# State space matrices prepared in six pieces on three engines, and all sines after the last table

## The chip, the cores and the metric

The kernel runs on one core of one Trainium2 chip. The metric is device time in microseconds for one launch, and the number given for the kernel is the median of several runs. Besides those runs there is one profiled execution, with its own time, from which every row below is taken.

## The reference

The reference is a network of two blocks over 256 tokens of width 1024, in float32. The first block has two layers, each a feed-forward part, a mixing part (two attentions and a pooling branch) and a second feed-forward part. The second block has an "even" layer with stick-breaking attention and a grouped state space mixer, and an "odd" layer with gated linear attention. Two parts matter here.

A feed-forward part (D_FF is 2816, so 22 chunks of 128 columns):

```
def swiglu(x, w_gate, w_up, w_down):
    return (jax.nn.silu(x @ w_gate) * (x @ w_up)) @ w_down
h = h + 0.5 * swiglu(rmsnorm(h, ffn2_norm[l]), ffn2_w_gate[l], ffn2_w_up[l], ffn2_w_down[l])
```

The parameters of the state space mixer, which depend on no token:

```
lam = lax.complex(lam_re, lam_im);  dt = jnp.exp(log_dt)[:, None]
lam_bar = jnp.exp(lam * dt)
b_bar = ((lam_bar - 1.0) / lam)[..., None] * bmat
```

## The kernel before, in words

Activations lie transposed: 128 features on the partitions, the 256 tokens in the free dimension. Every weight is fetched in tiles of 128x1024 float32, two per transfer of 1 MB on SyncE's queue (`ahead`, L295, three buffers named raw). `W` (L302) splits each tile for the matmuls: ScalarE copies it to the rounded format (L313, tile wh), VectorE writes the rest, source minus wh (L314, tile wl). Six buffers of wh and of wl let the split run ahead of TensorE. A product is then three matmuls (`mm3`, L317): high by high (L319), high by low (L320), low by high (L321).

`ffn` (L525) goes over the 22 chunks f. For a chunk, TensorE projects the gate and the up columns into one PSUM tile, psa for even f and psb for odd f, 24 matmuls each. Then a short chain makes the hidden chunk: VectorE multiplies the gate by the token scale (L581), ScalarE applies SiLU (L582), GpSimd multiplies by the halved scale (L583), VectorE multiplies by the up part (L584), and `split` makes the high (L332, ScalarE) and low (L333, VectorE) halves, tile hs. One chunk later TensorE multiplies hs by the down weights, 24 matmuls into psc. So a chunk is 72 matmuls on TensorE: the down product of chunk f-1, and the two projections of chunk f+1. Below, "the down product of chunk f" is named D and the number: D8 is that of chunk 8. It cannot start before L332 of chunk f has written hs.

In the last feed-forward part (f21), `ffn` also calls one step of a list at the head of each chunk from f = 1: `s5_prep` (L955) returns that list. It prepares what the even layer needs and what depends on parameters alone:

- `begin` (f = 1): three transfers and small columns of 128x16.
- `table` (f = 2 to 9): a table of angles, two groups at a time. VectorE L997 and L998, GpSimd L999, VectorE L1000, GpSimd L1001 and L1002, VectorE L1003 and L1004. Every second one ends with an absolute value on ScalarE (L1006), and its 512 columns are then a finished quarter of the table.
- `sines` (f = 10): three small sines (L1010 to L1012), the sine and cosine of each quarter (L1015, L1016), and a row of dependent 128x16 operations on GpSimd (L1017 to L1039), which give the columns cr, ci, lr and li.
- `outs` and `ins` (f = 11 and 12): 128x512 products of the matrices C and B with these columns, all on GpSimd (L1054 to L1086).
- `turned` (f = 13): eight transposes on TensorE (L1096) and two copies on ScalarE (L1097). `direct` (f = 14): 32 small matmuls (L1108, L1109) and four copies (L1112).

The order on an engine is not the order of the calls: a scheduler lists the instructions by their priority (the order of the calls) and by when it expects their inputs to be ready. Each engine then runs its own list strictly in that order, and an instruction that waits holds up all behind it on its engine. `issue_after` keeps what is traced in its block behind a given instruction of the same engine.

Of the kernel before, what the change touches and what calls it, by code (L numbers as in the profile page):

```python
# [12 lines left out]
AF = mybir.ActivationFunctionType  # L13
ALU = mybir.AluOpType
# [226 lines left out]
class Kern:  # L241
# [713 lines left out]
    def s5_prep(self):  # L955

        nc = self.nc
        g = nc.gpsimd
# [4 lines left out]
        tabs = []  # L963
        self.rho = rho2

        def view(t, m):
            return t.rearrange("p a t -> p (a t)").rearrange("p (m i t) -> p m i t", m=2, i=4)[:, m]
# [21 lines left out]
        def table(i):  # L989

            if i % 4 == 0:
                tabs.append(self.slot())
            sn = self.sin(i, 2).rearrange("p i t -> p (i t)")
            u, v, w = self.tmp(), self.tmp(), self.tmp()
            for m in range(2):
                h = slice(m * P, m * P + P)
                nc.vector.tensor_scalar(u[:, h], self.c("tidx"), ph[:, i + m:i + m + 1], None, ALU.mult)  # L997
                nc.vector.tensor_scalar(v[:, h], self.c("tidx"), pl[:, i + m:i + m + 1], None, ALU.mult)  # L998
            g.tensor_tensor(w, u, v, ALU.add)  # L999
            nc.vector.tensor_scalar(w, w, MAGIC, MAGIC, ALU.add, ALU.subtract)  # L1000
            g.tensor_tensor(u, u, w, ALU.subtract)  # L1001
            g.tensor_tensor(u, u, v, ALU.add)  # L1002
            nc.vector.tensor_scalar(u, u, 2 * math.pi, PI, ALU.mult, ALU.min)  # L1003
            nc.vector.tensor_scalar(sn, u, -PI, None, ALU.max)  # L1004
            if i % 4 == 2:
                nc.scalar.activation(view(tabs[-1], 1), view(tabs[-1], 0), AF.Abs)  # L1006

        def sines():
            with self.tc.issue_after(self.act.ins):
                nc.scalar.activation(sb, y, AF.Sin)  # L1010
                nc.scalar.activation(cb, ny, AF.Sin, bias=self.c("hpi"), scale=-1.0)
                nc.scalar.activation(sh, y, AF.Sin, scale=0.5)  # L1012
            for t in tabs:
                sn, cs = view(t, 0), view(t, 1)
                nc.scalar.activation(sn, sn, AF.Sin)  # L1015
                nc.scalar.activation(cs, cs, AF.Sin, bias=self.c("hpi"), scale=-1.0)  # L1016
            g.tensor_tensor(rho2, ea, ea, ALU.mult)  # L1017
            g.tensor_tensor(lr, ea, cb, ALU.mult)
            g.tensor_tensor(li, ea, sb, ALU.mult)

            g.tensor_scalar(em, ea, 1.0, None, ALU.add)
            g.tensor_tensor(em, em, th, ALU.mult)
            g.tensor_tensor(re, em, cb, ALU.mult)
            g.tensor_tensor(sh, sh, sh, ALU.mult)
            g.tensor_scalar(sh, sh, 2.0, None, ALU.mult)
            g.tensor_tensor(re, re, sh, ALU.subtract)
            g.tensor_tensor(im, ea, sb, ALU.mult)
            g.tensor_tensor(den, lre, lre, ALU.mult)
            g.tensor_tensor(t1, lim, lim, ALU.mult)
            g.tensor_tensor(den, den, t1, ALU.add)  # L1030
            nc.vector.reciprocal(den, den)
            g.tensor_tensor(cr, re, lre, ALU.mult)
            g.tensor_tensor(t1, im, lim, ALU.mult)
            g.tensor_tensor(cr, cr, t1, ALU.add)
            g.tensor_tensor(cr, cr, den, ALU.mult)
            g.tensor_tensor(ci, im, lre, ALU.mult)
            g.tensor_tensor(t1, re, lim, ALU.mult)
            g.tensor_tensor(ci, ci, t1, ALU.subtract)
            g.tensor_tensor(ci, ci, den, ALU.mult)  # L1039

        def wide(t):
            return t.rearrange("p a t -> p (a t)").rearrange("p (m i q) -> p m i q", m=2, i=16)

        def tile32():
            return self.tmp(512).rearrange("p (i q) -> p i q", i=16)

        def over(col):
            return col.unsqueeze(2).to_broadcast([P, 16, 32])

        def outs():  # L1050

            c0 = wide(self.s5c)
            t, t2 = tile32(), tile32()
            g.tensor_tensor(t, c0[:, 0], over(ci), ALU.mult)  # L1054
            g.tensor_tensor(t2, c0[:, 1], over(ci), ALU.mult)
            g.tensor_tensor(c0[:, 0], c0[:, 0], over(cr), ALU.mult)
            g.tensor_tensor(c0[:, 1], c0[:, 1], over(cr), ALU.mult)
            g.tensor_tensor(c0[:, 0], c0[:, 0], t2, ALU.subtract)
            g.tensor_tensor(c0[:, 1], c0[:, 1], t, ALU.add)
            g.tensor_scalar(c0[:, 1], c0[:, 1], -1.0, None, ALU.mult)  # L1060
            cs = [self.slot().rearrange("p a t -> p (a t)").rearrange("p (m i q) -> p m i q", m=2, i=16)
                  for _ in range(2)]
            neg, one, two, three = cs[0][:, 0], cs[0][:, 1], cs[1][:, 0], cs[1][:, 1]
            g.tensor_scalar(neg, c0[:, 0], -1.0, None, ALU.mult)
            t, t2 = tile32(), tile32()
            g.tensor_tensor(t, c0[:, 1], over(li), ALU.mult)
            g.tensor_tensor(t2, c0[:, 0], over(li), ALU.mult)
            g.tensor_tensor(one, c0[:, 0], over(lr), ALU.mult)
            g.tensor_tensor(two, c0[:, 1], over(lr), ALU.mult)
            g.tensor_tensor(one, one, t, ALU.add)  # L1070
            g.tensor_tensor(two, two, t2, ALU.subtract)
            g.tensor_scalar(three, one, -1.0, None, ALU.mult)
            self.cp = (one, two, three), (c0[:, 0], c0[:, 1], neg)

        def ins():

            n0 = wide(self.s5n)
            self.s5l = self.slot()
            l0 = wide(self.s5l)
            t, t2 = tile32(), tile32()  # L1080
            g.tensor_tensor(t, n0[:, 1], over(li), ALU.mult)
            g.tensor_tensor(t2, n0[:, 0], over(li), ALU.mult)
            g.tensor_tensor(l0[:, 0], n0[:, 0], over(lr), ALU.mult)
            g.tensor_tensor(l0[:, 1], n0[:, 1], over(lr), ALU.mult)
            g.tensor_tensor(l0[:, 0], l0[:, 0], t, ALU.subtract)
            g.tensor_tensor(l0[:, 1], l0[:, 1], t2, ALU.add)  # L1086

        def turned():

# [10 lines left out]
        def direct():  # L1100
# [11 lines left out]
                nc.scalar.activation(kt[q, :, q], ps[q].rearrange("p (c d) -> p c d", c=4), AF.Copy)  # L1112
            self.kt = kt

        return [begin] + [lambda i=i: table(i) for i in range(0, 16, 2)] + [sines, outs, ins, turned, direct]

    def even(self, h):

# [511 lines left out]
```

## Time and profile before

| what | value |
|---|---|
| runs | 1625.89, 1628.82, 1629.08 us; median 1628.82 us |
| profiled execution, its own time | 1626.93 us |
| its span, first to last instruction | 1625.2 us |
| VectorE, ScalarE, GpSimd busy | 64%, 50%, 24% of the span |
| mean granted TensorE clock | 0.994 |

The span is what the rows are drawn from; 1.73 us of the execution lie around it. In the rows TensorE is PE, VectorE DVE, ScalarE ACT and GpSimd POOL. Times in a timeline are from the span's start. The last feed-forward part lies at about 1060 to 1285 us, and the matrices are prepared in it.

### The profile page before, as it was taken

How to read it: one execution, taken by the hardware profiler on the slowest of the kernel's cores; microseconds unless marked ns; L12 is line 12 of the kernel's file. 1: busy time of each engine (PE TensorE's matmuls, PEld its weight loads, DVE VectorE, ACT ScalarE, POOL GpSimd, SP SyncE). 2: the span in 40 equal slices, each digit the busy share in tenths (PEclk: the TensorE clock that was granted, in tenths of full speed). 3: DMA queues.
4: the chain of work that ended last, by engine and by line, in shares of the span. 5: the costliest groups of instructions: out<-in, count | busy, mean ns of one | idle time of the engine just before them, and what ended most of it. 6: DMA issues, size and time to landing. Idle time of an engine off the chain costs nothing. (4 is left out here: it accounts for less than half of the span.)

```text
span 1625.2 us, 30427 instructions
## 1 busy us (share of the span) xinstructions
PE 1578.4 (97%) x12518; PEld 1506.2 (93%) x12518; DVE 1044.4 (64%) x1725; ACT 817.8 (50%) x1412; POOL 385.1 (24%) x446
## 2 busy tenths in 40 slices
PE   8999999999999999999999999999869999999998
PEld 8999998999999999999999899999869987998886
DVE  6655576676765557555576576776545687677643
ACT  6444455555544445444455565454434544566663
POOL 3111142002411113111141000453551111112232
PEclk9999999999999999999999999999989999999999
DMA  7555543334355554455544343554524433442530
GB/s 277 193 184 179 182 176 126 142 132 167 144 209 181 186 184 176 182 182 182 182 163 156 130 150 137 182 195 156 178 95 177 174 130 132 145 164 81 182 130 27
DMA packets 38459, 261.97 MB, mean 161 GB/s; under 512 B 4336, under 2 KB 5616, under 8 KB 7344
## 3 DMA queue, kind: packets, MB, share of 16 engines
q1 hardware_dynamic: 37440, 257.61, 44.1%
q0 software_dynamic: 736, 2.34, 0.5%
q8 instruction: 98, 1.61, 0.4%
q14 instruction: 41, 0.34, 0.1%
q10 hardware_dynamic: 144, 0.08, 0.0%
HBM read 258.96 MB, written 1.05 MB: 160 GB/s over the span
## 5 line engine op out<-in xcount | busy, mean ns | idle before, releaser
L314 DVE TENSOR_TENSOR wl<-raw,wh 128x1024 fp32r<-128x1024 f32 (+1 forms) x487 | 605.8, 1249 | 247.5 <-ACT wh L313 246.6
L313 ACT ACTIVATE wh<-raw 128x1024 fp32r<-128x1024 f32 (+1 forms) x487 | 508.2, 1049 | 449.2 <-PE psa L320 210.6
L319 PE MATMUL psa<-s,wh 128*128 128x256 f32 x1800 | 516.7, 288 | 2.0 <-ACT s L335 0.9
L320 PE MATMUL psa<-s,wh 128*128 128x256 f32 x1800 | 513.1, 285 | 4.9 <-DVE s L336 4.4
L321 PE MATMUL psa<-s,wl 128*128 128x256 f32 x1800 | 510.9, 284 | 0.2 <-DVE wl L314 0.2
L320 PEld LDWEIGHTS psa<-s,wh 128*128 128x128 f32 x1800 | 344.9, 192 | 11.1 <-DVE s L336 9.3
L319 PEld LDWEIGHTS psa<-s,wh 128*128 128x128 f32 x1800 | 344.6, 192 | 10.6 <-issue 5.4
L321 PEld LDWEIGHTS psa<-s,wl 128*128 128x128 f32 x1800 | 344.9, 192 | 2.0 <-issue 1.5
L583 POOL TENSOR_TENSOR t<-t,hrb 128x256 f32<-128x256 f32 x88 | 121.7, 1382 | 525.1 <-ACT t L582 525.1
L319 PE MATMUL psc<-hs,wh 128*128 128x256 f32 x704 | 200.7, 287 | 20.8 <-ACT hs L332 20.8
L319 PE MATMUL psb<-s,wh 128*128 128x256 f32 x752 | 213.9, 284 | 0.1
L321 PE MATMUL psb<-s,wl 128*128 128x256 f32 x752 | 213.2, 283 | 0.0
L320 PE MATMUL psb<-s,wh 128*128 128x256 f32 x752 | 213.1, 283 | 0.0
L320 PE MATMUL psc<-hs,wh 128*128 128x256 f32 x704 | 202.2, 288 | 2.9 <-DVE hs L333 2.1
L321 PE MATMUL psc<-hs,wl 128*128 128x256 f32 x704 | 200.5, 285 | 0.0
L319 PEld LDWEIGHTS psc<-hs,wh 128*128 128x128 f32 x704 | 136.0, 194 | 23.1 <-ACT hs L332 23.0
L319 PEld LDWEIGHTS psb<-s,wh 128*128 128x128 f32 x752 | 144.4, 192 | 0.6 <-ACT s L1097 0.3
L320 PEld LDWEIGHTS psb<-s,wh 128*128 128x128 f32 x752 | 144.4, 192 | 0.0
L321 PEld LDWEIGHTS psb<-s,wl 128*128 128x128 f32 x752 | 144.4, 192 | 0.0
L320 PEld LDWEIGHTS psc<-hs,wh 128*128 128x128 f32 x704 | 136.5, 194 | 5.9 <-DVE hs L333 5.8
L321 PEld LDWEIGHTS psc<-hs,wl 128*128 128x128 f32 x704 | 136.6, 194 | 0.0
L332 ACT ACTIVATE hs<-t 128x256 fp32r<-128x256 f32 x88 | 36.6, 416 | 166.2 <-DVE t L584 166.0
(382 smaller groups left out, 2146.0 us busy)
## 6 DMA issues: line engine op xcount, KB each, us to landing
raw<-in_w SPq DMA_DIRECT2D x242, 1024.0 KB, 4.8
s<-in_x SPq DMA_DIRECT2D x4, 256.0 KB, 5.7
raw<-in_w SPq DMA_DIRECT2D x4, 256.0 KB, 6.4
out<-t SPq DMA_DIRECT2D x8, 128.0 KB, 1.8
cst<-in_cst SPq DMA_DIRECT2D x1, 545.5 KB, 7.2
sq<-in_pw POOLq DMA_DIRECT2D x2, 256.0 KB, 3.8
s<-in_s5b POOLq DMA_DIRECT2D x1, 512.0 KB, 3.5
s<-in_s5c POOLq DMA_DIRECT2D x1, 512.0 KB, 3.8
```

The source lines that it names most:

```text
L313: self.act = nc.scalar.activation(hi[:, s], src[:, s], AF.Copy)
L314: nc.vector.tensor_tensor(lo[:, s], src[:, s], hi[:, s].bitcast(F32), ALU.subtract)
L319: mm(ps, wh, xh, start=start, stop=False, skip_group_check=True)
L320: mm(ps, wh, xl, start=False, stop=False, skip_group_check=True)
L321: return mm(ps, wl, xh, start=False, stop=stop, skip_group_check=True)
L332: nc.scalar.activation(hi, src, AF.Copy)
L583: nc.gpsimd.tensor_tensor(sg, sg, hrb, ALU.mult)
```

## The change

What was one step for the C matrices (`outs`) and one for the B matrices (`ins`), both wholly on GpSimd, becomes six steps. Each of the three matrix results is begun in one step and ended in the next. In a `begin` step VectorE makes three 128x512 products and GpSimd one; in an `end` step VectorE and GpSimd combine one half each, and ScalarE takes over two of the three sign changes (the third is folded into a VectorE operation). The transposes and the small matmuls come later, at f = 18 and f = 20, with an empty step ahead of each. The sines of the four quarters now wait, with the three small sines, for the last absolute value of the tables.

```diff
             if i % 4 == 2:
-                nc.scalar.activation(view(tabs[-1], 1), view(tabs[-1], 0), AF.Abs)
+                self.abs = nc.scalar.activation(view(tabs[-1], 1), view(tabs[-1], 0), AF.Abs)
 
         def sines():
-            with self.tc.issue_after(self.act.ins):
+            with self.tc.issue_after(self.abs.ins):
                 nc.scalar.activation(sb, y, AF.Sin)
                 nc.scalar.activation(cb, ny, AF.Sin, bias=self.c("hpi"), scale=-1.0)
                 nc.scalar.activation(sh, y, AF.Sin, scale=0.5)
-            for t in tabs:
-                sn, cs = view(t, 0), view(t, 1)
-                nc.scalar.activation(sn, sn, AF.Sin)
-                nc.scalar.activation(cs, cs, AF.Sin, bias=self.c("hpi"), scale=-1.0)
+                for t in tabs:
+                    sn, cs = view(t, 0), view(t, 1)
+                    nc.scalar.activation(sn, sn, AF.Sin)
+                    nc.scalar.activation(cs, cs, AF.Sin, bias=self.c("hpi"), scale=-1.0)
...
-        def outs():
+        def begin_outs():
 
             c0 = wide(self.s5c)
-            t, t2 = tile32(), tile32()
-            g.tensor_tensor(t, c0[:, 0], over(ci), ALU.mult)
-            g.tensor_tensor(t2, c0[:, 1], over(ci), ALU.mult)
-            g.tensor_tensor(c0[:, 0], c0[:, 0], over(cr), ALU.mult)
-            g.tensor_tensor(c0[:, 1], c0[:, 1], over(cr), ALU.mult)
-            g.tensor_tensor(c0[:, 0], c0[:, 0], t2, ALU.subtract)
-            g.tensor_tensor(c0[:, 1], c0[:, 1], t, ALU.add)
-            g.tensor_scalar(c0[:, 1], c0[:, 1], -1.0, None, ALU.mult)
...
+            w["t"], w["t2"] = tile32(), tile32()
+            v.tensor_tensor(w["t"], c0[:, 0], over(ci), ALU.mult)
+            g.tensor_tensor(w["t2"], c0[:, 1], over(ci), ALU.mult)
+            v.tensor_tensor(c0[:, 0], c0[:, 0], over(cr), ALU.mult)
+            v.tensor_tensor(c0[:, 1], c0[:, 1], over(cr), ALU.mult)
+
+        def end_outs():
+            c0 = wide(self.s5c)
+            g.tensor_tensor(c0[:, 0], c0[:, 0], w["t2"], ALU.subtract)
+            v.scalar_tensor_tensor(c0[:, 1], c0[:, 1], -1.0, w["t"], ALU.mult, ALU.subtract)
+
+        def begin_ahead():
...
+            nc.scalar.activation(neg, c0[:, 0], AF.Copy, scale=-1.0)
+            v.tensor_tensor(w["t"], c0[:, 1], over(li), ALU.mult)
+            g.tensor_tensor(w["t2"], c0[:, 0], over(li), ALU.mult)
+            v.tensor_tensor(one, c0[:, 0], over(lr), ALU.mult)
+            v.tensor_tensor(two, c0[:, 1], over(lr), ALU.mult)
+
+        def end_ahead():
...
+            v.tensor_tensor(one, one, w["t"], ALU.add)
+            g.tensor_tensor(two, two, w["t2"], ALU.subtract)
+            nc.scalar.activation(three, one, AF.Copy, scale=-1.0)
...
-        return [begin] + [lambda i=i: table(i) for i in range(0, 16, 2)] + [sines, outs, ins, turned, direct]
+        return [begin] + [lambda i=i: table(i) for i in range(0, 16, 2)] + [
+            sines, begin_outs, end_outs, begin_ahead, end_ahead, begin_ins, end_ins, lambda: None, turned,
+            lambda: None, direct]
```

`begin_ins` and `end_ins` do for `ins` what `begin_outs` and `end_outs` do for `outs`: three products and one combination on VectorE, one of each on GpSimd. In the changed file the new lines have numbers from 1050 on: L1056 to L1059 are `begin_outs`, L1063 and L1064 `end_outs`, L1072 to L1076 `begin_ahead`, L1081 to L1083 `end_ahead`, L1092 to L1095 `begin_ins`, L1099 and L1100 `end_ins`. Outside the last feed-forward part every engine's list is as it was.

ScalarE, at the second absolute value of the tables (L1006, in the chain of chunk 5), as one piece of the difference:

```order
 L313 ACTIVATE wh<-raw 128x1024 x2
 L1006 ACTIVATE s<-s 128x512
-L1015 ACTIVATE s<-s 128x512
-L1016 ACTIVATE s<-s,cst 128x512
 L313 ACTIVATE wh<-raw 128x1024
 L582 ACTIVATE t<-t 128x256
```

The sine and cosine of the quarter leave the place between the absolute value and the SiLU of the chunk (L582); so it is in chunk 7 too. All four pairs stand now behind the fourth L1006, in the chain of chunk 9, in the order L1010, L1011, L1012, L1015, L1016, L1015, L582, L1016, L1015, L332, L1016, L1015, L1016.

GpSimd, from the last two of the small columns (L1038, L1039) on, before:

```order
L1038 TENSOR_TENSOR s5p<-s5p 128x16
L1039 TENSOR_TENSOR s5p<-s5p 128x16
L1001 TENSOR_TENSOR t<-t 128x256
L1002 TENSOR_TENSOR t<-t 128x256
L583 TENSOR_TENSOR t<-t,hrb 128x256
L999 TENSOR_TENSOR t<-t 128x256
L1001 TENSOR_TENSOR t<-t 128x256
L1002 TENSOR_TENSOR t<-t 128x256
L583 TENSOR_TENSOR t<-t,hrb 128x256 x2
L1054 TENSOR_TENSOR t<-s,s5p 128x512
L1055 TENSOR_TENSOR t<-s,s5p 128x512
L1056 TENSOR_TENSOR s<-s,s5p 128x512
```

and now:

```order
L1038 TENSOR_TENSOR s5p<-s5p 128x16
L1039 TENSOR_TENSOR s5p<-s5p 128x16
L583 TENSOR_TENSOR t<-t,hrb 128x256 x2
L1057 TENSOR_TENSOR t<-s,s5p 128x512
L1063 TENSOR_TENSOR s<-s,t 128x512
L583 TENSOR_TENSOR t<-t,hrb 128x256 x2
L1074 TENSOR_TENSOR t<-s,s5p 128x512
L1082 TENSOR_TENSOR s<-s,t 128x512
L583 TENSOR_TENSOR t<-t,hrb 128x256 x2
L1093 TENSOR_TENSOR t<-s,s5p 128x512
L1100 TENSOR_TENSOR s<-s,t 128x512
L583 TENSOR_TENSOR t<-t,hrb 128x256 x7
```

The row of small columns has moved from the middle of the seventh table to behind the last one; the first L583 behind it is that of chunk 9. The seventeen matrix operations that stood between the L583 of chunk 10 and that of chunk 11 are now three pairs, with two L583 between them.

VectorE, from chunk 10 (psa) to the first product of chunk 11 (L581 of psb), before:

```order
L581 TENSOR_TENSOR t<-psa,rb 128x256
L314 TENSOR_TENSOR wl<-raw,wh 128x1024
L584 TENSOR_TENSOR t<-t,psa 128x256
L333 TENSOR_TENSOR hs<-t,hs 128x256
L314 TENSOR_TENSOR wl<-raw,wh 128x1024 x2
L581 TENSOR_TENSOR t<-psb,rb 128x256
```

and now:

```order
L584 TENSOR_TENSOR t<-t,psa 128x256
L1056 TENSOR_TENSOR t<-s,s5p 128x512
L333 TENSOR_TENSOR hs<-t,hs 128x256
L1058 TENSOR_TENSOR s<-s,s5p 128x512
L1059 TENSOR_TENSOR s<-s,s5p 128x512
L314 TENSOR_TENSOR wl<-raw,wh 128x1024
L1064 SCALAR_TENSOR_TENSOR s<-s,t 128x512
L1075 TENSOR_TENSOR s<-s,s5p 128x512
L1076 TENSOR_TENSOR s<-s,s5p 128x512
L314 TENSOR_TENSOR wl<-raw,wh 128x1024
L581 TENSOR_TENSOR t<-psb,rb 128x256
```

Six of the twelve matrix operations that VectorE takes over stand in this one chunk; the other six come in chunks 11, 12 and 14, two each. L1075 reads what GpSimd writes in L1063.

## Rows read from the trace of the kernel before

**Rows 1.** The page, busy time of each engine, with its share and instructions.
```profile
PE 1578.4 (97%) x12518; PEld 1506.2 (93%) x12518; DVE 1044.4 (64%) x1725; ACT 817.8 (50%) x1412; POOL 385.1 (24%) x446
```
**Rows 2.** Two stretches: length, busy time of PE, PEld, DVE, ACT, POOL, granted clock, DMA.
```profile
1151.10:1155.20 4.10, 3.99 (x18) 3.80 (x19) 2.42 (x5) 1.86 (x2) 1.95 (x3) 0.59 0.41 144
1180.00:1200.00 20.00, 5.90 (x32) 5.36 (x32) 8.10 (x7) 3.87 (x6) 17.32 (x15) 0.66 0.07 24
```
**Rows 3.** Timeline of PE, first matmuls of down products: start, length, instruction, wait before.
```profile
1099.87 0.28 PE L319 MATMUL psc<-hs,wh 128*128 128x256 f32 x1
...
1109.40 0.28 PE L319 MATMUL psc<-hs,wh 128*128 128x256 f32 x1
...
1138.66 0.38 PE L319 MATMUL psc<-hs,wh 128*128 128x256 f32 x1 [1.44 <-ACT hs L332]
...
1151.12 0.39 PE L319 MATMUL psc<-hs,wh 128*128 128x256 f32 x1 [3.21 <-ACT hs L332]
...
1170.87 0.28 PE L319 MATMUL psc<-hs,wh 128*128 128x256 f32 x1
...
1191.51 0.58 PE L319 MATMUL psc<-hs,wh 128*128 128x256 f32 x1 [11.84 <-ACT hs L332]
...
1200.28 0.39 PE L319 MATMUL psc<-hs,wh 128*128 128x256 f32 x1 [2.07 <-ACT hs L332]
...
1216.45 0.28 PE L319 MATMUL psc<-hs,wh 128*128 128x256 f32 x1
...
1225.09 0.28 PE L319 MATMUL psc<-hs,wh 128*128 128x256 f32 x1
...
1233.73 0.28 PE L319 MATMUL psc<-hs,wh 128*128 128x256 f32 x1
```
**Rows 4.** Timeline of POOL: the small columns and the matrices.
```profile
1140.06 1.20 POOL L1019 TENSOR_TENSOR s5p<-s5p 128x16 f32<-128x16 f32 x1
...
1144.59 0.22 POOL L1039 TENSOR_TENSOR s5p<-s5p 128x16 f32<-128x16 f32 x1
...
1167.12 1.05 POOL L1054 TENSOR_TENSOR t<-s,s5p 128x512 f32<-128x512 f32 x1
...
1173.37 2.28 POOL L1058 TENSOR_TENSOR s<-s,t 128x512 f32<-128x512 f32 x1
...
1189.83 0.72 POOL L583 TENSOR_TENSOR t<-t,hrb 128x256 f32<-128x256 f32 x1
```
**Rows 5.** Timeline of ACT: high halves of hidden chunks (L332), a sine, an absolute value.
```profile
1107.62 0.42 ACT L332 ACTIVATE hs<-t 128x256 fp32r<-128x256 f32 x1 [1.71 <-DVE t L584]
...
1118.34 0.42 ACT L332 ACTIVATE hs<-t 128x256 fp32r<-128x256 f32 x1 [2.04 <-DVE t L584]
...
1127.50 0.42 ACT L332 ACTIVATE hs<-t 128x256 fp32r<-128x256 f32 x1 [1.70 <-DVE t L584]
...
1150.65 0.42 ACT L332 ACTIVATE hs<-t 128x256 fp32r<-128x256 f32 x1 [1.69 <-DVE t L584]
...
1156.13 0.63 ACT L1006 ACTIVATE s<-s 128x512 f32<-128x512 f32 x1 [3.17 <-DVE s L1004]
```
**Rows 6.** Timeline of DVE: two chunk products, and three waits or slow operations.
```profile
1104.99 0.42 DVE L581 TENSOR_TENSOR t<-psa,rb 128x256 f32<-128x256 f32 x1
...
1107.17 0.42 DVE L584 TENSOR_TENSOR t<-t,psa 128x256 f32<-128x256 f32 x1 [0.63 <-POOL t L583]
...
1116.03 1.23 DVE L314 TENSOR_TENSOR wl<-raw,wh 128x1024 fp32r<-128x1024 f32 x1 [1.46 <-ACT wh L313]
...
1146.36 0.30 DVE L1003 TENSOR_SCALAR t<-t 128x256 f32<-128x256 f32 x1 [4.94 <-POOL t L1002]
...
1169.04 3.46 DVE L314 TENSOR_TENSOR wl<-raw,wh 128x1024 fp32r<-128x1024 f32 x2 [0.52 <-ACT wh L313]
```
**Rows 7.** DVE by line and form, of 1050 to 1400 us: busy us, mean ns, idle.
```profile
L1266 DVE TENSOR_TENSOR t<-t,s 128x512 f32<-128x512 f32 x16 | 11.0, 689 | 0.3
```
**Rows 8.** Timeline of PE: the eight transposes.
```profile
1197.17 1.04 PE L1096 MATMUL psb<-cst,s 128*128 128x128 f32 x8
```

More of the change, by code (lines that the diff above doesn't have):

```diff
@@ L1042, in wide @@
             return t.rearrange("p a t -> p (a t)").rearrange("p (m i q) -> p m i q", m=2, i=16)
+        w, v, halves = {}, nc.vector, wide
         def tile32():
@@ L1048, in over @@
             return col.unsqueeze(2).to_broadcast([P, 16, 32])
-        def outs():
+        def begin_outs():
             c0 = wide(self.s5c)
-            t, t2 = tile32(), tile32()
-            g.tensor_tensor(t, c0[:, 0], over(ci), ALU.mult)
-            g.tensor_tensor(t2, c0[:, 1], over(ci), ALU.mult)
-            g.tensor_tensor(c0[:, 0], c0[:, 0], over(cr), ALU.mult)
-            g.tensor_tensor(c0[:, 1], c0[:, 1], over(cr), ALU.mult)
-            g.tensor_tensor(c0[:, 0], c0[:, 0], t2, ALU.subtract)
-            g.tensor_tensor(c0[:, 1], c0[:, 1], t, ALU.add)
-            g.tensor_scalar(c0[:, 1], c0[:, 1], -1.0, None, ALU.mult)
[L1061 to L1072, printed above, removed]
@@ new lines, in begin_ahead @@
+        def begin_ahead():
+            c0 = wide(self.s5c)
+            w["c"] = (neg, one, two, three) = [
+                t[:, m] for t in (halves(self.slot()), halves(self.slot())) for m in range(2)]
+            w["t"], w["t2"] = tile32(), tile32()
+            nc.scalar.activation(neg, c0[:, 0], AF.Copy, scale=-1.0)
[3 more added lines that the diff above has]
+            v.tensor_tensor(two, c0[:, 1], over(lr), ALU.mult)
@@ L1073, in outs, with begin_ins @@
+        def end_ahead():
+            c0 = wide(self.s5c)
+            neg, one, two, three = w["c"]
+            v.tensor_tensor(one, one, w["t"], ALU.add)
+            g.tensor_tensor(two, two, w["t2"], ALU.subtract)
+            nc.scalar.activation(three, one, AF.Copy, scale=-1.0)
             self.cp = (one, two, three), (c0[:, 0], c0[:, 1], neg)
-        def ins():
+        def begin_ins():
             n0 = wide(self.s5n)
@@ L1079, in ins, with end_ins @@
             l0 = wide(self.s5l)
[L1080 to L1086, printed above, removed]
+            w["t"], w["t2"] = tile32(), tile32()
+            v.tensor_tensor(w["t"], n0[:, 1], over(li), ALU.mult)
+            g.tensor_tensor(w["t2"], n0[:, 0], over(li), ALU.mult)
+            v.tensor_tensor(l0[:, 0], n0[:, 0], over(lr), ALU.mult)
+            v.tensor_tensor(l0[:, 1], n0[:, 1], over(lr), ALU.mult)
+        def end_ins():
+            l0 = wide(self.s5l)
+            v.tensor_tensor(l0[:, 0], l0[:, 0], w["t"], ALU.subtract)
+            g.tensor_tensor(l0[:, 1], l0[:, 1], w["t2"], ALU.add)
         def turned():
```

## Prediction

> **What bounds the kernel now.** I read the page first: TensorE is busy for 1578.4 of 1625.2 us [rows 1], so only the 47 us in which it is not can be won without less work. Then a table by stage: in 1180 to 1200 us TensorE works for 5.90 of 20 us while GpSimd is busy for 17.32, and the granted clock is 0.66 [rows 2]. That is the last feed-forward part, where the change lies. Third, the timeline of TensorE there. At rest a chunk takes 1233.73 - 1225.09 = 8.64 us [rows 3]. From D3 at 1099.87 to D13 at 1216.45 there are ten chunks, which would be 86.4 us; they take 116.58. So 30.2 us are lost: D3 to D4 0.9, D4 to D7 3.3, D7 to D8 3.8, D8 to D10 2.5, D10 to D11 12.0, D11 to D13 7.7, each the difference of the starts less 8.64 per chunk. The waits all name L332, the high half of the hidden chunk. Fourth, what holds L332: the queue of GpSimd. From 1167.12 on it works through the matrix operations, and L583 of chunk 11 gets its turn at 1189.83 [rows 4].
>
> **What a late L332 costs.** D8 starts at 1151.12, 0.46 us after L332 at 1150.65 [rows 3, 5]; the low half is later still, and a down product that has waited takes some 0.3 to 0.4 us more. A wait has a second price. After the wait of 3.21 us the granted clock is 0.59 in the next 4.1 us [rows 2, 3], so mostly the lower level of 1.2 GHz: 4.1 x (1 - 0.59) = 1.7 us are lost. After the wait of 1.44 us at 1138.66 the product keeps its pace, so somewhere between the two the clock falls.
>
> **The change, step by step.** I go along the chunks on the old time axis.
>
> *Sines leave the table chunks.* L332 comes 10.72 us after the one before in a chunk with an absolute value (1107.62 to 1118.34) and 9.16 us in one without (to 1127.50) [rows 5]. The difference is ScalarE's queue: L314 waits 1.46 us for its wh behind the sine and the cosine [rows 6]. Without them both kinds should take 9.16. From 1107.62, chunks 5 to 8 then have L332 at 1116.8, 1125.9, 1135.1 and 1144.2. TensorE wants them at 1118.0, 1126.7, 1135.3 and 1144.5 (1109.40 plus 8.64 each, with what was lost). With the 0.46 us between L332 and the product, D7 waits about 0.2 us. D4 to D7 loses 0.2 us instead of 3.3.
>
> *The small columns leave the seventh table.* They hold GpSimd from 1140.06 to 1144.81, so L1003 waits 4.94 us on VectorE [rows 4, 6] and D8 3.21 us. That goes: D7 to D8 loses 0.5 us instead of 3.8.
>
> *The small columns return behind the eighth table.* There L583 of chunk 9 stands behind them. L1006 follows L332 by 5.48 us (1150.65 to 1156.13), so it comes at 1149.7, lasts 0.63, and the first small sine lets the columns begin at about 1150.5. They take 4.75 us if L1019 lasts 1.20 us again, 3.8 if it lasts 0.22 as L1039 does [rows 4]. L583 then runs for 0.72 us to 1155.0 or 1156.0, L332 follows L584 by 0.45 (1107.17 to 1107.62), and D9 starts at 1156.0 to 1156.9, where TensorE was ready at 1153.6. I take 2.9 us of wait plus the 0.3 of D8: D8 to D9 loses 3.2. The clock may or may not fall; half of 1.7 us, and 0.4 for the late low half, make 1.2 for D9 to D10. So D8 to D10 loses 4.4 us instead of 2.5. The eight sines, some 0.63 us each as L1006, lie beside this: ScalarE would wait for L583 in that time anyway, and TensorE still has split tiles in hand. If it had none, their 5 us less the 2.9 already counted would come on top.
>
> *The matrices.* Seventeen operations go from between two L583; a pair on GpSimd takes 1.05 to 2.28 us each [rows 4] and has two chunks to itself. VectorE's twelve 128x512 operations are not in the trace with these operands. The nearest row is L1266, as wide and with one repeated operand: 0.69 us [rows 7]. From below, half of the 1.23 us of a 1024-wide L314 [rows 6] is 0.62; from above, twice the 0.69 is 1.38, since GpSimd's own operations go from 1.05 to over 2 when VectorE works beside them. I take 0.69. The six that stand in one chunk decide. After L332 of chunk 10: 0.88 for its low half, L1058 and L1059 1.38, L314 1.23, three more 2.07, L314 1.23, L581 0.42, L1094 0.69, L314 1.23, then L584 and 0.45 to L332: 9.6 us, where 8.64 are free and the reserve is about 0.5. While L1057 and L1063 run beside it, L314 is slower: two of them took 3.46 instead of 2.46 us beside the old matrix operations [rows 6]. That makes 10.1 us, and D11 about 1.0 us late: D10 to D11 loses 1.0 instead of 12.0. L314 waits behind this burst, and TensorE for it; but wl runs up to six tiles ahead, 2.88 us each, which covers a burst of 4. If the tiles were not ahead, its 4 us would stand on TensorE's path. The other six come two to a chunk and are covered by the idle time of VectorE (64% busy [rows 1]). ScalarE's two copies cost about as much as L1006, 0.63 us each, beside 50% idle time.
>
> The Trainium skill, in "SBUF — State Buffer", section "Who interferes with whom", says that VectorE with two SBUF inputs and GpSimd share one interface, and that the later one is blocked for the whole of the other's instruction. The slow L314 agrees with it in kind. By that rule GpSimd's L583, L1057 and L1063 would hold VectorE for up to 3 us, where I took 0.5; D11 would be 2.5 us later.
>
> *Transposes and small matmuls.* The eight transposes take 1.04 us [rows 8], the small matmuls less; they are paid before and after. In the old order the transposes came just behind the long wait, with another wait of 2.07 us [rows 3] and the lower clock: these go with it. With 1.9 us for both and 0.4 for the late low half of D11, D11 to D13 and the later place lose 2.3 instead of 7.7.
>
> **The sum.** After: 0.9 + 0.2 + 0.5 + 4.4 + 1.0 + 2.3 = 9.3 us, before 30.2, so 20.9 us are won. From the profiled execution's 1626.93 us that makes 1606.0. The median of the runs is 1.9 us above that execution, which would give 1607.9. I predict 1607.
>
> **Rivals.**
>
> A, *nothing is left to wait for*: the columns run at 0.2 us each beside an idle VectorE, so that D9 is not late enough to matter, and the burst hides in the split tiles. Then only 0.9 and 1.9 remain, 27.4 us are won: 1599.5 to 1601.4. Against it stands that 3.8 us of columns are more than D9's reserve. Chance 0.13.
>
> B, *the burst becomes the bound of its chunk*: VectorE's operations take 1.38 us, D11 comes 4 to 5 us later, its wait and that of D9 both let the clock fall. That adds about 8 us: 1615. For it speaks the slow L314, against it L1266 at 0.69. Chance 0.18.
>
> C, *slower*: VectorE's queue stops at the matrix operations that read GpSimd's results, with L314 and L581 behind them, as L1003 did for 4.94 us [rows 6]. If such a stop comes at chunks 11 to 17, each costs what the one before D8 did: 3.2 of wait, 1.7 of clock, 0.4 for the low half, some 5.3 us. Four of them eat the gain, all seven make 37 us: 1643. Against it: only L1075 reads a result of GpSimd of the same chunk, the other pieces have a chunk between. Chance 0.04.
>
> D, *the pieces don't part*: VectorE takes half of them in one chunk already; should the long wait only move from GpSimd to VectorE, the time stays within 0.2%. But 12 operations of 0.69 are 8 us in all, not 22. Chance 0.05.
>
> **How the numbers follow.** The forecast has 0.60, for 1602 to 1612 by its own bounds (each unknown at its better or worse end). A and B belong within the range, C and D without: 1600 to 1616. A measurement of this kernel can tell about 0.2%, or 3.3 us, from no change. Faster by more than that are the forecast, A and B: 0.91; within it D: 0.05; slower C: 0.04.
>
> **What would show it.** Right: the wait of 11.84 us and that of 3.21 us are gone from TensorE's timeline, L332 comes every 9.2 us through chunks 4 to 8, a wait of 2 to 4 us stands before D9 with the columns in front of L583, and one of about 1 us before D11. D18's stretch shows the transposes without a wait behind them. Wrong: L314 on VectorE later than the matmul that reads it, a wait of over 3 us before D11 to D17, or a clock below 0.9 in more than one stretch of 20 us. It would also be wrong if the feed-forward part were shorter by 20 us and the even layer longer: its lists are the same, so nothing there should give time back.

## The result, and the profile after

The changed kernel takes 1607.38 us (median of four runs, 1606.15 to 1609.65), the kernel before 1628.84 us on the same chip (1625.89 to 1629.08). The ratio is 0.9874, with a 95% interval of 0.9857 to 0.9891. The prediction was 1607.0 us. The profiled execution is the longest of the four, 1609.65 us; its span is 1608.0 us.

The page's busy line:

```profile
PE 1578.2 (98%) x12518; PEld 1504.7 (94%) x12518; DVE 1050.6 (65%) x1737; ACT 819.0 (51%) x1414; POOL 363.3 (23%) x431
```

Two stretches of the view by windows, with the columns of [rows 2]:

```profile
1156.10:1160.20 4.10, 4.01 (x21) 3.81 (x22) 1.83 (x3) 4.10 (x6) 0.00 (x0) 0.66 0.00 0
...
1180.00:1200.00 20.00, 20.00 (x169) 20.00 (x169) 16.10 (x19) 9.81 (x15) 9.13 (x7) 1.00 0.59 211
```

Beside [rows 1], GpSimd has lost 22 us and VectorE gained 6; TensorE's busy time is the same, so only its waits can have gone. Beside [rows 2], TensorE now works through all of 1180 to 1200 us, at the full clock, where it worked 5.90 of 20. The timeline of TensorE: the first matmuls of D3, D4 and D6 to D12, then the transposes, D18, and the first projection behind the small matmuls:

```profile
1099.34 0.28 PE L319 MATMUL psc<-hs,wh 128*128 128x256 f32 x1
...
1108.87 0.28 PE L319 MATMUL psc<-hs,wh 128*128 128x256 f32 x1
...
1126.16 0.38 PE L319 MATMUL psc<-hs,wh 128*128 128x256 f32 x1
...
1135.60 0.38 PE L319 MATMUL psc<-hs,wh 128*128 128x256 f32 x1 [0.18 <-ACT hs L332]
...
1144.77 0.38 PE L319 MATMUL psc<-hs,wh 128*128 128x256 f32 x1
...
1156.11 0.39 PE L319 MATMUL psc<-hs,wh 128*128 128x256 f32 x1 [2.10 <-ACT hs L332]
...
1166.67 0.28 PE L319 MATMUL psc<-hs,wh 128*128 128x256 f32 x1
...
1176.24 0.39 PE L319 MATMUL psc<-hs,wh 128*128 128x256 f32 x1 [0.77 <-ACT hs L332]
...
1185.33 0.28 PE L319 MATMUL psc<-hs,wh 128*128 128x256 f32 x1
...
1222.77 1.34 PE L1110 MATMUL psb<-cst,s 128*128 128x128 f32 x8
...
1238.35 0.28 PE L319 MATMUL psc<-hs,wh 128*128 128x256 f32 x1
...
1242.10 0.39 PE L319 MATMUL psa<-s,wh 128*128 128x256 f32 x1
```

The wait of 11.84 us and that of 3.21 us [rows 3] are gone; one of 2.10 us before D9 is new, one of 0.77 us stands before D11. With 8.64 us a chunk taken off the starts, as in the prediction:

| stretch | lost before | predicted | lost after |
|---|---|---|---|
| D3 to D4 | 0.9 | 0.9 | 0.9 |
| D4 to D7 | 3.3 | 0.2 | 0.8 |
| D7 to D8 | 3.8 | 0.5 | 0.5 |
| D8 to D10 | 2.5 | 4.4 | 4.6 |
| D10 to D11 | 12.0 | 1.0 | 0.9 |
| D11 on, with transposes and small matmuls | 7.7 | 2.3 | 2.5 |
| sum, of the unrounded numbers | 30.2 | 9.3 | 10.3 |

The last row after is 0.45 for D11 to D12, 1.18 for the transposes (D12 to D18 less six times 8.64; their row has grown from 1.04 [rows 8] to 1.34 us) and 0.87 for the small matmuls (the next product would start 2.88 us after D18 without them, and starts 3.75 after). So 19.9 us are won where 20.9 were predicted.

The rest is outside the change. Against 1626.93 us of the profiled execution before, 19.9 us and a start of D3 that is 0.5 us earlier make 1606.5, not 1609.65. The missing 3.1 us are lost in the odd layer, whose instructions are the same. Two stretches of 5 us there, in the view by windows of this execution:

```profile
1565.00:1570.00 5.00, 3.35 (x18) 1.71 (x17) 1.77 (x4) 1.77 (x7) 1.91 (x4) 1.00 0.00 0
1570.00:1575.00 5.00, 5.00 (x14) 2.18 (x13) 1.10 (x4) 2.46 (x8) 2.77 (x7) 0.54 0.01 3
```

The same two in another execution of the same kernel, which took 1606.21 us ("changed again" below):

```profile
1565.00:1570.00 5.00, 3.35 (x18) 1.90 (x18) 1.38 (x4) 2.06 (x7) 1.77 (x5) 1.00 0.00 0
1570.00:1575.00 5.00, 5.00 (x27) 3.06 (x26) 1.64 (x5) 3.35 (x13) 3.61 (x7) 1.00 0.02 3
```

TensorE does the same work up to 1570 us in both, with a wait of 1.4 us at the end of it. Then the clock falls in one execution (0.54, so nearly the lower level of 1.2 GHz) and not in the other. From this wait to the next one on the same line the first takes 16.28 us and the second 13.20, so the whole 3.1 us lie there. From the start of D18 to the end of the span the first takes 1608.0 - 1238.35 = 369.65 us, the second 1604.5 - 1237.93 = 366.57. So the median's distance of 0.4 us from the forecast says little: the four runs lie 3.5 us apart, and like for like 1606.0 were forecast for an execution that took 1609.65.

### The profile page after: what moved, and what is told of

Its sections match the earlier page's. It is cut to its first block, busy times and chain, and to the rows that moved or that the text cites. A ratio compares the mean times of both kernels' runs of the same rounds, so it can differ in the third digit from the quotient of the medians.

```text
span 1608.0 us, 30431 instructions
## 1 busy us (share of the span) xinstructions
PE 1578.2 (98%) x12518; PEld 1504.7 (94%) x12518; DVE 1050.6 (65%) x1737; ACT 819.0 (51%) x1414; POOL 363.3 (23%) x431
## 4 chain that ended last, share of the span: by engine, by line
PE 84%; DVE 6%; POOL 4%; ACT 3%; issue 2%; DMA 0%; SPq 0%; DVEq 0%; ACTq 0%; POOLq 0%
PE psa L319 12%; PE psa L320 12%; PE psa L321 12%; PE psc L320 6%; PE psc L321 6%; PE psc L319 6%; PE psb L319 5%; PE psb L320 5%; PE psb L321 5%; DVE s L336 1%; DVE wl L314 1%; ACT wh L313 1%; PE psb L636 1%; PE psa L636 1%; PE psa L638 1%
## 5 line engine op out<-in xcount | busy, mean ns | idle before, releaser
L314 DVE TENSOR_TENSOR wl<-raw,wh 128x1024 fp32r<-128x1024 f32 (+1 forms) x487 | 602.8, 1243 | 240.8 <-ACT wh L313 238.2
L583 POOL TENSOR_TENSOR t<-t,hrb 128x256 f32<-128x256 f32 x88 | 121.6, 1382 | 521.1 <-ACT t L582 521.1
L332 ACT ACTIVATE hs<-t 128x256 fp32r<-128x256 f32 x88 | 36.6, 416 | 153.0 <-DVE t L584 152.9
```

Of the source, the lines that this page charges most:

```text
L314: nc.vector.tensor_tensor(lo[:, s], src[:, s], hi[:, s].bitcast(F32), ALU.subtract)
L332: nc.scalar.activation(hi, src, AF.Copy)
L583: nc.gpsimd.tensor_tensor(sg, sg, hrb, ALU.mult)
```

## The experiments

All are timed against the kernel before on the same chip: 1626.99 us for the first four, 1627.09 for the next four, 1626.34 for the last two. Two of them are repeats, of the changed kernel and of the best one. The table puts them in the order of the wait before D11. The middle columns count the matrix operations on GpSimd between L583 of chunk 10 and of chunk 11, and those on VectorE between L584 of the two. A second number in the last column is a wait inside the product, for the low half.

| kernel | median, us | GpSimd | VectorE | wait in D11, us |
|---|---|---|---|---|
| sines only | 1624.82 | 17 | 0 | 14.14 |
| before | 1627 | 17 | 0 | 11.84 |
| six steps, all on GpSimd | 1617.18 | 12 | 0 | 8.24 |
| shared, large steps | 1613.16 | 4 | 10 | 3.74 + 1.99 |
| columns early | 1604.74 | 2 | 7 | 1.17 |
| changed again | 1606.38 | 2 | 7 | 1.04 |
| pieces only | 1608.31 | 2 | 7 | 0 |
| vector spread | 1606.70 | 2 | 3 | 0 |
| both edits | 1603.31, again 1605.12 | 2 | 3 | 0 |
| both, VectorE alone | 1602.98 | 0 | 4 | 0 |

### Sines only

```diff
 (before)
-            with self.tc.issue_after(self.act.ins):
+            with self.tc.issue_after(self.abs.ins):
...
-            for t in tabs:
-                sn, cs = view(t, 0), view(t, 1)
+                for t in tabs:
+                    sn, cs = view(t, 0), view(t, 1)
```

> The kernel before with one part of the change alone: all sines, the two large pairs too, wait for the last absolute value of the tables. The matrices are made as before, in three steps by GpSimd. My theory is that the waits of this stretch hang on each other: with the sines in one place the wait of 3.2 us before chunk 8's hidden product goes and the wait of 2 us before chunk 9's comes, but GpSimd's 17 operations for the matrices still stand ahead of L583 of chunk 11, so that this product waits about 11 to 14 us as before. Time: 1626 us (1625 to 1627), two to three us below the kernel before. The rival theory, that the gains of the parts add up, counts only the waits before chunks 7, 8 and 9 (3.3 + 3.3 - 1.9 = 4.7 us) and gives 1624.

Measured: 1624.82 us, ratio 0.9987 (0.9979 to 0.9996). That is just below my 1625 to 1627, but the kernel before is 1.9 us faster here than in the result. As a difference it is 2.2 us (0.7 to 3.4), my theory's two to three and not the rival's 4.7. The trace shows why. D11 in TensorE's timeline:

```profile
1188.03 0.58 PE L319 MATMUL psc<-hs,wh 128*128 128x256 f32 x1 [14.14 <-ACT hs L332]
```

GpSimd's timeline, the last of the seventeen operations and L583 of chunk 11:

```profile
1185.34 1.05 POOL L1084 TENSOR_TENSOR s<-s,s5p 128x512 f32<-128x512 f32 x1
1186.35 0.72 POOL L583 TENSOR_TENSOR t<-t,hrb 128x256 f32<-128x256 f32 x1
```

D9 waits 2.13 us, as expected, D8 not at all, and D11 waits 2.3 us longer than before: what the front of the stretch wins is in part waited for again behind GpSimd.

### Pieces only

```diff
 (changed)
-            with self.tc.issue_after(self.abs.ins):
+            with self.tc.issue_after(self.act.ins):
...
-                for t in tabs:
-                    sn, cs = view(t, 0), view(t, 1)
+            for t in tabs:
+                sn, cs = view(t, 0), view(t, 1)
```

> The other part alone: the six pieces, shared among the three engines, with the sines of before (the two large pairs not held back). My theory: chunk 11's hidden product waits less than 1 us where it waited 11.8, chunks 11 to 13 lose nothing, the wait of 3.2 us before chunk 8's product stays and the one before chunk 9's is not there. The gain is about 17.6 us, the time 1610 to 1611.5. The rival, that the pieces only do this together with the sines' new place (since otherwise the first piece still meets the small columns on GpSimd), has 3 to 5 us of wait left before chunks 10 and 11 and a time of 1613 to 1616.

Measured: 1608.31 us, ratio 0.9886 (0.9871 to 0.9902). The gain is 18.7 us, nearly all of it; the rival falls. My 1610 to 1611.5 was too high (I had a gain of about 17.6 us), and my expectation was wrong in two places. TensorE's timeline at D7, D8, D9 and D11:

```profile
1137.92 0.38 PE L319 MATMUL psc<-hs,wh 128*128 128x256 f32 x1 [1.44 <-ACT hs L332]
...
1150.36 0.38 PE L319 MATMUL psc<-hs,wh 128*128 128x256 f32 x1 [1.70 <-ACT hs L332]
...
1161.05 0.39 PE L319 MATMUL psc<-hs,wh 128*128 128x256 f32 x1 [1.45 <-ACT hs L332]
...
1178.77 0.28 PE L319 MATMUL psc<-hs,wh 128*128 128x256 f32 x1
```

D8 waits 1.70 us and not 3.2, and D9 does wait. But D7 to D8 is 12.44 us here and 12.46 before [rows 3]: the starts are the same, only the wait is shorter, since in this execution the clock fell during D7. That stretch in the view by windows:

```profile
1137.92:1142.02 4.10, 4.01 (x21) 3.81 (x22) 2.43 (x5) 3.20 (x6) 3.24 (x9) 0.66 0.57 230
```

The same stretch of the kernel before:

```profile
1138.66:1142.76 4.10, 4.00 (x31) 3.81 (x32) 2.44 (x5) 3.21 (x6) 3.23 (x9) 1.00 0.60 236
```

Both stand behind a wait of 1.44 us. Where the next product waits for the other engines in any case, a slow clock only fills the wait. So it was before, too: D8 to D9 is 10.69 us in both, but there D8 ran at the lower clock, which hid the wait that D9 has here.

From D3 to D10 this kernel takes 71.03 us, as the kernel before does (71.00); the changed kernel takes 67.33. So the sines' new place wins 3.7 us there. From D10 to D18 the changed kernel takes 1.4 us longer (71.68 against 70.29), since the same operations on VectorE find less reserve before D11: D10 starts 1.83 us behind L332 there and 3.24 here. The sines are worth 2.3 us by the traces, 0.9 to 1.9 by the medians.

### Six steps, all on GpSimd

```diff
 (changed; each of the three begin steps, and so in the end steps)
-            v.tensor_tensor(w["t"], c0[:, 0], over(ci), ALU.mult)
+            g.tensor_tensor(w["t"], c0[:, 0], over(ci), ALU.mult)
```

> The changed kernel with its six steps, but every operation of the matrices on GpSimd, as before the change. It tells the two halves of the second part apart: steps or sharing. If sharing among the engines decides, GpSimd has about twelve operations of 1 to 2 us between its parts of chunks 10 and 11, chunk 11's hidden product waits about 6 us and the clock falls behind it: 1614 to 1616 us. If it is the six steps that decide, no wait above 2 us is left and the time is that of the changed kernel, 1607 to 1608.

Measured: 1617.18 us, ratio 0.9946 (0.9933 to 0.9958). The six steps alone don't do it: D11 waits 8.24 us where I had about 6, and the time lies above my 1614 to 1616. GpSimd's timeline, the first and the last operation of its run and L583 of chunk 11:

```profile
1163.52 1.05 POOL L1056 TENSOR_TENSOR t<-s,s5p 128x512 f32<-128x512 f32 x1
...
1179.31 1.05 POOL L1096 TENSOR_TENSOR s<-s,s5p 128x512 f32<-128x512 f32 x1
1180.32 0.72 POOL L583 TENSOR_TENSOR t<-t,hrb 128x256 f32<-128x256 f32 x1
```

The scheduler put twelve operations, of four steps whose calls are up to four chunks apart, between two L583; with 16.8 us they hold it up. Steps in the source are not yet steps on the engine.

### Shared, in large steps

```diff
 (changed)
-            sines, begin_outs, end_outs, begin_ahead, end_ahead, begin_ins, end_ins, lambda: None, turned,
-            lambda: None, direct]
+            sines, lambda: (begin_outs(), end_outs(), begin_ahead(), end_ahead()),
+            lambda: (begin_ins(), end_ins()), lambda: None, lambda: None, lambda: None, lambda: None,
+            lambda: None, turned, lambda: None, direct]
```

> The changed kernel with its sharing among the engines, but in steps as large as before: the four pieces for the outputs and for the chunk ahead are one step, the two for the inputs another. If sharing decides, GpSimd has only four operations between two of its feed-forward parts and VectorE about seven more, chunk 11's hidden product comes 1 to 2.5 us later than in the changed kernel, and the time is 1608 to 1610. If the six steps decide, the wait before it is again over 6 us and the time 1614 or more.

Measured: 1613.16 us, ratio 0.9916 (0.9902 to 0.9929). My 1608 to 1610 fails, and so do the rival's wait of over 6 us and its 1614, narrowly (waits of 3.74 and 1.99). VectorE's timeline, L584 of chunk 10, the end of the run up to L584 of chunk 11, and the operation behind it:

```profile
1163.92 0.42 DVE L584 TENSOR_TENSOR t<-t,psa 128x256 f32<-128x256 f32 x1 [0.63 <-POOL t L583]
...
1174.72 1.21 DVE L1095 TENSOR_TENSOR s<-s,s5p 128x512 f32<-128x512 f32 x1
1175.86 2.06 DVE L314 TENSOR_TENSOR wl<-raw,wh 128x1024 fp32r<-128x1024 f32 x1
1177.84 0.41 DVE L584 TENSOR_TENSOR t<-t,psb 128x256 f32<-128x256 f32 x1
1178.17 1.42 DVE L1092 TENSOR_TENSOR t<-s,s5p 128x512 f32<-128x512 f32 x1
```

There are ten, not seven, so that the two L584 are 13.92 us apart. L584 of chunk 11 stands right behind L314 and doesn't wait for GpSimd. This is the prediction's rival B, VectorE's burst as the bound of its chunk, here with ten operations. With the sines in their new place, sharing without splitting wins 13.8 us, splitting without sharing 9.8, both together 20.7: neither half explains it alone.

### The changed kernel again, and three edits on it

> The changed kernel once more, beside the three that follow, so that differences under one per cent are read on one chip: 1607.4 us, within 0.1%.

Measured: 1606.38 us (1606.21 to 1609.63), ratio 0.9877 (0.9860 to 0.9893).

*Columns early:*

```diff
 (changed)
+            if i == 4:
+                small()
...
-            g.tensor_tensor(u, u, v, ALU.add)
+            last = g.tensor_tensor(u, u, v, ALU.add)
+            if i in (8, 12):
+                with self.tc.issue_after(last.ins):
+                    columns(i)
```

The new `small` makes the three small sines and the columns that read none of them, `columns` the others in two halves; `sines` keeps the large sines.

> The changed kernel, but the three small sines come with the table of chunk 4, and the small columns on GpSimd in two halves behind the tables of chunks 6 and 8, so that none of them is left between chunk 8's projections and chunk 9's product. My theory: the 2.1 us wait before chunk 9's product comes from GpSimd's L583 standing behind the 3.85 us of columns; it goes, up to a rest of about 1 us (ScalarE still has large sines ahead of L582), and 2 to 3 us are gained: 1604.5 (1603.5 to 1605.5). The rival says that ScalarE's run of sines holds chunk 9 by itself, so that nothing is gained: 1607.

Measured: 1604.74 us (1604.43 to 1609.75). D9 waits 0.77 us in place of 2.15, and D18 starts 1.4 us earlier than in the changed kernel (1236.52 against 1237.93); D11 waits a little longer, 1.17 us, and D8 waits 0.72 us where it waited for nothing. The time is as expected, though by the trace less than the 2 to 3 us are won. The columns on GpSimd did hold D9, by 1.4 us; the rest is the rival's, since L582 of chunk 9 stands right behind large sines there. Behind L582, as in "both" below, they leave a wait of 0.19.

*Vector spread:*

```diff
 (changed)
-            nc.vector.tensor_tensor(hf, sg, pu, ALU.mult)
+            self.hf = nc.vector.tensor_tensor(hf, sg, pu, ALU.mult)
...
+        def behind(step):
+            with self.tc.issue_after(self.hf.ins):
+                step()
...
-            sines, begin_outs, end_outs, begin_ahead, end_ahead, begin_ins, end_ins, lambda: None, turned,
+            sines] + [lambda f=f: behind(f) for f in (
+                begin_outs, end_outs, begin_ahead, end_ahead, begin_ins, end_ins)] + [lambda: None, turned,
```

> The changed kernel, but each of the six steps' operations is held behind the latest L584 on VectorE, so that they are spread over chunks 10 to 15 in place of a run of seven ahead of chunk 11's hidden activations. Where this run makes chunk 11's product late, the wait of 0.77 us goes and 0.9 to 1.3 us are gained: 1606.3. The rival: this wait comes from GpSimd's L583 (which VectorE slows down), and nothing changes: 1607.4.

Measured: 1606.70 us (1604.73 to 1607.48): by the time, no difference. By the trace the wait is gone and D18 starts at 1235.98, 1.95 us earlier than in the changed kernel again. TensorE's timeline at D11:

```profile
1174.27 0.28 PE L319 MATMUL psc<-hs,wh 128*128 128x256 f32 x1
```

But the profiled execution (1607.27 us) lost 3 us in the odd layer again, 369.6 us from D18 to its end. The burst was the cause of D11's wait; the gain is smaller than what the odd layer takes in some runs.

*Both*, and the large sines held behind L582 of chunk 9:

```diff
 (columns early and vector spread, and:)
-            with self.tc.issue_after(self.abs.ins):
+            with self.tc.issue_after(self.silu.ins):
```

> Both edits together, and the large sines on ScalarE held behind L582 of chunk 9 as well. If the waits before chunks 9 and 11 are separate, no wait over 0.3 us is left between chunks 9 and 18 and the time is the changed kernel's less 4 to 5 us: 1602.5 to 1603.5. If the gain of chunk 9 is lost again at chunk 11, because everything arrives there earlier, 1605 or more.

Measured: 1603.31 us (1602.61 to 1606.24), ratio 0.9855 (0.9840 to 0.9869). TensorE's timeline at D9, at D10's second group of matmuls and at D11:

```profile
1154.23 0.38 PE L319 MATMUL psc<-hs,wh 128*128 128x256 f32 x1 [0.19 <-ACT hs L332]
...
1164.41 0.38 PE L320 MATMUL psc<-hs,wh 128*128 128x256 f32 x1 [0.60 <-DVE hs L333]
...
1173.01 0.28 PE L319 MATMUL psc<-hs,wh 128*128 128x256 f32 x1
```

The gains are separate: 3.2 us at D18 (1234.72), where the two edits alone have 1.4 and 1.95. That is less than the 4 to 5 us expected, though the time lies in the range. It is faster than the kernel before. Against the changed kernel only the trace carries the statement: the repeat below has a ratio of 0.9872, which is that of the changed kernel (0.9874 and 0.9877). The 0.60 us is VectorE's L1068, the first matrix operation, ahead of the low half, and more than the 0.3 that I had allowed; L1068 takes 1.19 us:

```profile
1162.83 1.19 DVE L1068 TENSOR_TENSOR t<-s,s5p 128x512 f32<-128x512 f32 x1
...
1165.48 2.31 DVE L314 TENSOR_TENSOR wl<-raw,wh 128x1024 fp32r<-128x1024 f32 x1
```

### VectorE alone

```diff
 (both; all six matrix operations of GpSimd)
-            g.tensor_tensor(w["t2"], c0[:, 1], over(ci), ALU.mult)
+            v.tensor_tensor(w["t2"], c0[:, 1], over(ci), ALU.mult)
```

> The kernel with both edits, but GpSimd's six operations of the matrices go to VectorE too, in the same places, so that VectorE has 18 and GpSimd none. It asks what GpSimd's share is worth. My theory: VectorE and GpSimd slow each other when they run side by side, so that what VectorE takes over (0.68 us each) it gets back: L1068 takes 0.68 in place of 1.18 us, the L314 of 2.31 us takes 1.2, and the wait of 0.60 us for the low half before the second matmul of chunk 10 shrinks to about 0.1. Time: that of the kernel with both edits, less 0.5 us at most. The rival, that VectorE needs the relief, has chunks 10 to 15 late by 0.7 us each and a time 2 to 4 us longer.

> The kernel with both edits once more, on the same chip as the one with VectorE alone: 1603.3 us, within 0.1%.

Measured: 1602.98 us (1602.41 to 1606.91) for VectorE alone, 1605.12 (1603.87 to 1607.60) for both edits again, which is 0.1% above its first time, on another chip. Ratios 0.9865 (0.9848 to 0.9881) and 0.9872 (0.9857 to 0.9887): no slower, and the rival's 2 to 4 us longer fall. VectorE's timeline in chunk 10, with VectorE alone:

```profile
1162.78 0.68 DVE L1068 TENSOR_TENSOR t<-s,s5p 128x512 f32<-128x512 f32 x1
...
1165.52 2.35 DVE L314 TENSOR_TENSOR wl<-raw,wh 128x1024 fp32r<-128x1024 f32 x2
```

L1068 takes 0.68 us where it took 1.19, two L314 take 2.35 where one took 2.31, and the wait of 0.60 us is gone. So VectorE does GpSimd's share in the time that it lost beside GpSimd. What matters is that little stands between two L583 and between two L584, not that three engines share.

## Why the prediction was right

**The long wait.** GpSimd's run in front of L583 of chunk 11 was the cause: with 17 operations there D11 waits 11.84 us (14.14 with the sines moved), with 12 it waits 8.24. With four or two, what is left follows VectorE's list: ten operations there make 3.74 and 1.99 us, seven about 1 us, or none where D10 itself comes later (pieces only), three none. That is the step on which 16 of the 20 us rest. The later place of the transposes and small matmuls, a part of the change, stands in every kernel here but sines only and was not tested alone.

**D4 to D7: 0.2 predicted, 0.8 measured.** ScalarE's timeline, L332 of chunks 5 to 8:

```profile
1116.53 0.42 ACT L332 ACTIVATE hs<-t 128x256 fp32r<-128x256 f32 x1 [1.98 <-DVE t L584]
...
1125.69 0.42 ACT L332 ACTIVATE hs<-t 128x256 fp32r<-128x256 f32 x1 [1.70 <-DVE t L584]
...
1135.13 0.42 ACT L332 ACTIVATE hs<-t 128x256 fp32r<-128x256 f32 x1 [1.98 <-DVE t L584]
...
1144.30 0.42 ACT L332 ACTIVATE hs<-t 128x256 fp32r<-128x256 f32 x1 [1.71 <-DVE t L584]
```

Predicted were 1116.8, 1125.9, 1135.1 and 1144.2; the interval of up to 10.72 us [rows 5] is now 9.44 at most, and D7 waited 0.18 us. What was missing: D6 starts right behind L332, as D7 does, and such a product takes 3.49 us, not 3.04, as its low half comes late; D6's 0.45 us count here. I had put that at 0.3 to 0.4 us, but only for products with a wait.

**D8 to D11: 5.4 predicted, 5.5 measured, for partly wrong reasons.** GpSimd's timeline: the first and last of the columns and L583 of chunk 9, then the first two matrix operations and L583 of chunk 11.

```profile
1150.62 0.36 POOL L1019 TENSOR_TENSOR s5p<-s5p 128x16 f32<-128x16 f32 x1 [1.50 <-ACT s5p L1010]
...
1154.26 0.22 POOL L1039 TENSOR_TENSOR s5p<-s5p 128x16 f32<-128x16 f32 x1
1154.43 0.72 POOL L583 TENSOR_TENSOR t<-t,hrb 128x256 f32<-128x256 f32 x1
...
1164.30 1.05 POOL L1057 TENSOR_TENSOR t<-s,s5p 128x512 f32<-128x512 f32 x1
1166.98 1.61 POOL L1063 TENSOR_TENSOR s<-s,t 128x512 f32<-128x512 f32 x1 [1.63 <-DVE s L1058]
1173.47 1.80 POOL L583 TENSOR_TENSOR t<-t,hrb 128x256 f32<-128x256 f32 x1 [4.89 <-ACT t L582]
```

The columns take 3.8 us (1150.62 to 1154.43), the lower bound [rows 4], and D8 to D9 loses 2.7 where I had 3.2. Then I added half of a fall of the clock. It fell (0.66, above), and cost nothing: in the spread kernel it did not fall behind the same wait, and L332 of chunk 10 follows that of chunk 9 by 9.19 us there and by 9.20 here. D11 waits for the chain of the other engines in either case; at full clock its wait of 0.77 would be some 1.4 us longer, an estimate (D9 to D10 takes 10.56 us here, 9.19 there). So the right price of the fall was nothing, and the sum of the stretch came out by luck. Nor does the clock fall somewhere between a wait of 1.44 us and one of 3.21, as I read from the trace before: behind 1.44 us it fell in pieces only, and behind 2.12 us it held in vector spread.

**The burst before D11.** VectorE's timeline in the changed kernel, from L584 of chunk 10 to that of chunk 11:

```profile
1164.38 0.42 DVE L584 TENSOR_TENSOR t<-t,psa 128x256 f32<-128x256 f32 x1 [0.63 <-POOL t L583]
1164.72 1.18 DVE L1056 TENSOR_TENSOR t<-s,s5p 128x512 f32<-128x512 f32 x1
...
1166.76 0.68 DVE L1059 TENSOR_TENSOR s<-s,s5p 128x512 f32<-128x512 f32 x1
1167.36 2.31 DVE L314 TENSOR_TENSOR wl<-raw,wh 128x1024 fp32r<-128x1024 f32 x1
...
1175.31 0.42 DVE L584 TENSOR_TENSOR t<-t,psb 128x256 f32<-128x256 f32 x1 [0.63 <-POOL t L583]
```

It takes 10.93 us, not 10.1: an operation is 0.68 us, as L1266 said [rows 7], but L1056 takes 1.18 and L314 2.31 beside GpSimd, and L583 1.80. The reserve was larger as well, 1.83 us from L332 to D10 less the 0.47 that a product needs behind it, so 1.36 and not 0.5. It comes from the slow clock, which kept D10 back: in vector spread, where the clock held, D10 starts 0.47 us behind L332 and there is none. 10.93 - 8.64 - 1.36 = 0.93 us, against 1.0: two errors that cancel, by luck.

I had set the Trainium skill's rule ("SBUF — State Buffer", section "Who interferes with whom") aside for 0.5 us. The trace agrees with it, nearly to the number: the one that starts later ends as if it had begun 0.13 us before the other's end. L1057 ends at 1165.35 and L1056 0.55 us after it, its own length being 0.68. L1063 ends at 1168.59 and L314 1.08 after it, its own being 1.22. A later L314 ends at 1174.68 and GpSimd's L583 0.59 after it, its own being 0.72. That is 0.50, 1.09 and, against L583's 1.14 in chunk 10, 0.66 us: 2.25 in all, where I had 0.5 and the rule up to 3. Without it the burst would be some 8.7 us, an estimate, and not my 9.6, since operations on VectorE follow each other every 0.60 us (1166.76 to 1167.36).

**The rivals.** A (nothing left) falls with D9's wait. Its 1599.5 to 1601.4 was not reached with more edits either, though VectorE alone comes within 2 us of it and both edits within 2 and 4. B did not come: VectorE's operations take 0.68 us, one of them 1.18 beside GpSimd, and not 1.38. Such a burst is seen in the kernel with large steps. C did not show: no product from D12 to D18 waits. D (the pieces don't part) did not come either; where they run together on GpSimd, 9.8 us are still won. The signs of being wrong did not show either: from D3 to 1285 us TensorE waits for no tile of L314, and of all stretches of 20 us one has a clock below 0.9 (0.83 at 1560 to 1580 us, in the odd layer).

## What to carry to other kernels

Where a side job shares its engines with a chain that the bound engine waits for, count what stands between two links of the chain in each engine's list, and keep it below the reserve; the number of steps in the source says little, as the scheduler can put them together again. Hold the pieces behind a link of the chain, one or two at a time. Spread on one engine with idle time, they may cost no more than shared with another that slows it.

## What the runs showed of the hardware

- A wait on TensorE of one length is followed by the lower clock in one execution and not in another: behind 2.10 to 2.15 us before D9 it fell in three executions (0.66, 0.61 and 0.58 in the next 4.1 us) and held in three (1.00, sines only, six steps on GpSimd, vector spread); behind 1.44 us it fell once (0.66) and held once (1.00). In pieces only, where it fell behind 1.44 us, it held behind 1.70 and 1.45 (1.00 both). What decides it these runs don't show.
- The same holds in the odd layer, with no edit near it. From D18 to the end of the span five executions take 366.6 us, one 368.1, and four 369.6 (changed, pieces only, six steps on GpSimd, vector spread). A kernel's spread of some 3 us from run to run, 1606.2 to 1609.6 here, is of this size.
